# A hybrid mixer and attention block: weights split three groups ahead with five buffers per part, merge biases on SyncE's queue, and three small products in other forms

## The chip, the cores and the metric

The kernel runs on 1 core of one Trainium2 chip. The metric is the device time of one execution in microseconds, the median of several runs. The engines are TensorE (PE; its weight loads are PEld), VectorE (DVE), ScalarE (ACT), GpSimd (POOL) and SyncE (SP), which issues most DMAs.

## The reference

One layer: an RMS-normalised input, one wide input projection, two branches (an RWKV-7 time mixer and a banded attention over chunks of 64), each gated by SiLU and projected, a merge by sigmoid gates with a bias, an output projection and a second norm. x is 256 x 2048, float32.

```python
h = _rms_norm(x, pre_norm_g[l])
proj = h @ w_in[l]                       # 2048 x 12288
p_r, p_k, p_v, z_r, q_a, k_a_att, v_a, z_a, m_r, m_a = jnp.split(proj, split_points, axis=-1)
y_r = _rwkv7_mixer(h, p_r, p_k, p_v, ...) * jax.nn.silu(z_r)
y_a = _chunk_band_attention(q_a, k_a_att, v_a, rel_bias[l]) * jax.nn.silu(z_a)
u_r = y_r @ w_branch_rwkv[l]
u_a = y_a @ w_branch_attn[l]
merged = (jax.nn.sigmoid(m_r + b_merge[l, 0]) * u_r
          + jax.nn.sigmoid(m_a + b_merge[l, 1]) * u_a)
x = x + _rms_norm(merged @ w_out[l], post_norm_g[l])
```

In the mixer a recurrence over 256 steps keeps, for each of 16 heads, a 64 x 64 state; it is decayed by w = exp(-0.606531 sigmoid(w0 + tanh(xw @ w1) @ w2)), and the rate a = sigmoid(a0 + (xa @ a1) @ a2) enters it.

## The kernel before, in words

**Weights.** Every big matrix is streamed in pieces of 512 KB: SP issues the load into one of NR = 3 buffers (tag raw, L90 and L97), ACT copies it to a rounded high part wh (L81), DVE subtracts to get the low part wl (L82). Both parts have their own rings of NH = NL = 4 buffers. A big product is the sum of three products of parts: L275 does them token by token, L339 (wh, 512 columns) and L337 (wl, 256 columns) do them with the two parts of the activations side by side. A step of the plan is one piece of one matrix; `run_plan` prepares (loads and splits) pieces up to step n + 2 before it emits the products of step n.

**Accumulators.** The big products have two (pool pm, tag mm, the acc_ names); the small ones share four (pool ps, tag sm). After a big product, `take` reads its accumulator: ACT the one half (L381), DVE the other (L382), and the accumulator is free when DVE is through.

**Small products.** The mixer and the attention are generators whose pieces are emitted between the steps of the plan. Heads go in duos (j0 = 0, 2, 4, 6) and two groups g of eight heads. `group_decay` makes the decay's product lw from zw (L452), `duo_front` makes for each duo and m the products pc (L500) and pa (L506, the rate a, with 64 rows) and then a chain of DVE operations (L511 to L536) that fills AB. The chunk loop of a group goes over four chunks c: pw (L647, and L651 with the state SB), its copy W on ACT (L653), the transposes pt with their copy BT (L658, L659; for c < 3), pu (L663), its copy UV on DVE and ACT (L665, L666), py and pg (L672, L677, L680), then SB from pg on DVE (L688, L690) and Y from py on ACT (L691). Tiles of a group share buffers with later ones: the tile `late` (takes of attention's later q and k) lies in the buffer of A (tag A), which py reads.

**Order.** Each engine works through its own list in order. The lists are made at build time by the framework's scheduler, which lays out the emitted instructions by its own timing; so a changed dependency or buffer count can move work far from the edited line. PE, DVE, ACT and SP wait in place for what their next instruction needs.

**Merge.** For each of four column blocks c and both branches w, `load_bias` loads a 256 KB bias tile bb (tag bb) on ACT's queue (L952); as tag bb had no earlier user, the first two loads are issued near the start.

Of the kernel before, what the change touches and what calls it, by code (L numbers as in the profile page):

```python
# [24 lines left out]
NR = 3  # L25
NH = 4
NL = 4

# [9 lines left out]
P = 128  # L38
D = 2048
# [22 lines left out]
def kernel(ctx: ExitStack, tc, x, xt, vecs, w_in, wa1, w2, a2, w0, rel, w_br, w_ba, w_out, post_g, bm, out):  # L62
# [214 lines left out]
    def run_plan():  # L277
# [20 lines left out]
        for n, (q, g) in enumerate(steps):  # L298
            while ready < len(steps) and ready <= n + 2:
                prepare(ready)  # L300
                ready += 1
# [62 lines left out]
    def normalise():  # L364
# [101 lines left out]
    def duo_front(j0):  # L466
# [30 lines left out]
        for m in range(2):  # L497
            pc = small(f"pc{j0}{m}")
            for i in range(2):
                PE.matmul(pc[:, i * 130:(i + 1) * 130], d["s"][:, i, (q0 + m) * P:(q0 + m + 1) * P],  # L500
                          cum.rearrange("p c t -> p (c t)"), start=True, stop=True)
            pcv = pc[:, 0:260].rearrange("p (c t) -> p c t", c=4)
            ACT.activation(pp[:, 4 * m:4 * m + 4, :], pcv, AF.Exp, scale=-DECAY)
            ACT.activation(iv[:, 4 * m:4 * m + 4, :], pcv[:, :, 1:65], AF.Exp, scale=DECAY)
            pa = small(f"pa{j0}{m}")
            PE.matmul(pa[:, :T], RA[0][64:128, DB + (j0 + m) * P:DB + (j0 + m + 1) * P], za[64:128, :], start=True, stop=True)  # L506
            ACT.activation(ta[:, m, :], pa[:, :T], AF.Tanh, scale=0.5, bias=col(hv, H_A0 + j0 + m))
            yield
# [55 lines left out]
    def group_back(g):  # L564
# [71 lines left out]
        for q in range(2):  # L636
            ACT.activation(Rq[q][0:32, :, 32:64], p4[q][0:32, 0:256].rearrange("p (u t) -> p u t", u=8), AF.Copy)
            DVE.tensor_copy(Rq[q][64:96, :, 32:64], p4[q][64:96, 0:256].rearrange("p (u t) -> p u t", u=8))
        yield
        Y = bg.tile([P, 4, 4, C], F32, tag=("Y", "v")[g], name=f"Y{g}")  # L640
        d["Y"] = Y
        for c in range(4):
# [10 lines left out]
            ACT.activation(W.rearrange("p j t -> p (j t)"), pw[:, 0:256], AF.Copy)  # L653
            if c < 3:
                BT = tp.tile([P, 4, P], F32, tag="BT", name=f"BT{g}{c}")
                pt = small(f"pt{g}{c}")
                for jj in range(4):
                    PE.transpose(pt[:, jj * P:(jj + 1) * P], AB[jj // 2][:, jj % 2, c, 2:4, :].rearrange("p a t -> p (a t)"), ident)  # L658
                ACT.activation(BT.rearrange("p j t -> p (j t)"), pt, AF.Copy)  # L659
            pu = small(f"pu{g}{c}")  # L660
# [12 lines left out]
            if c < 3:  # L673
                pg = small(f"pg{g}{c}")
                for jj in range(4):
                    for h in range(2):
                        PE.matmul(pg[HS[h], jj * C:(jj + 1) * C], BT[:, jj, HS[h]], UV[:, h, jj, c, :], start=True, stop=True)  # L677
            for jj in range(4):
# [132 lines left out]
    def attend(j0, q, k, z):  # L811
# [32 lines left out]
        for m in range(2):  # L844
            j = j0 + m
            S = att[0][:, 2 * m:2 * m + 2, :]
            Pt = []
            for h in range(2):
                pT = small(f"pT{j}{h}")
                for b in range(3):  # L850
                    PE.transpose(pT[:, b * P:(b + 1) * P], S[:, h, b * P:(b + 1) * P], ident)
                t = att[1][:, 2 * m + h, :]
                ACT.activation(t, pT[:, 0:384], AF.Copy)
                Pt.append(t)
            yield
            po = small(f"po{j}")
            for h in range(2):
                vc = slice((2 * j + h) * C, (2 * j + h + 1) * C)
                PE.matmul(po[HS[h], 0:256], va[0][:, vc], Pt[h][:, 0:256], start=True, stop=False)
            for h in range(2):  # L860
                vc = slice((2 * j + h) * C, (2 * j + h + 1) * C)
                PE.matmul(po[HS[h], 128:256], va[1][:, vc], Pt[h][:, 256:384], start=False, stop=True)
            yg = tp.tile([P, T], F32, tag="rn", name=f"ya{j}", bufs=1)
            DVE.scalar_tensor_tensor(yg, po[:, :T], 0.5, z[:, m, :], op0=ALU.mult, op1=ALU.mult)
            split(ya[j // 4][:, j % 4, 0, :], ya[j // 4][:, j % 4, 1, :], yg)
            yield

# [30 lines left out]
    def project_za(j0):  # L898
        def done(acc):
            if j0 < 4:  # L900
                z = tp.tile([P, 2, T], F32, tag="BT" if j0 else "zs", name=f"za{j0}", bufs=2 if j0 else 1)
            else:
                z = place(2 + j0 // 2)
# [171 lines left out]
```

## Time and profile before

| | us |
|---|---|
| median of 3 runs | 866.53 (866.11 to 867.91) |
| the profiled execution | 866.37 |
| its span, first to last instruction | 864.7 |
| PE busy | 847.0 (98%) |
| DVE busy | 571.4 (66%) |
| ACT busy | 424.7 (49%) |
| POOL busy | 16.7 (2%) |
| chain of waits that ended last | PE 94%, DVE 2%, DMA 2%, ACT 1%, issue 1% |

The profiled execution's mean granted clock is 0.991. The largest waits of PE by the list of waits are 1.6 us each for a high part of r (near 10 us) and before lw (73 us), 1.3 for SB, 1.3 for a low part of the lora weights and 1.2 for W; everything else is below 1. In rows of the timeline, a row may stand for several instructions of one form ("x16"): its time is from the first one's start to the last one's end, and ends overlap the next row's start, so steps are measured from start to start.

### The profile page before, as it was taken

What the parts mean: (1) busy time and instruction counts of PE and PEld (TensorE: products, weight loads), DVE (VectorE), ACT (ScalarE), POOL (GpSimd) and SP (SyncE); (2) the same over time, 40 slices, a digit from 0 to 9 for tenths busy, and PEclk for the clock granted to TensorE, in tenths of its full rate; (3) what the DMA queues carried; (4) which work ended last, traced back from release to release, by engine and by line L of the source; (5) the groups of instructions that cost most, each with busy time, mean ns of one, the idle gap of its engine ahead of it and who ended that gap; (6) DMA issues with size and microseconds to landing.
All of it is one profiled execution on the core that took longest, in us unless ns stands there. A gap on an engine that the chain in (4) does not pass through costs nothing.

```text
span 864.7 us, 14000 instructions
## 1 busy us (share of the span) xinstructions
PE 847.0 (98%) x5624; PEld 716.0 (83%) x5624; DVE 571.4 (66%) x801; ACT 424.7 (49%) x600; POOL 16.7 (2%) x66
## 2 busy tenths in 40 slices
PE   8999999999999999999999999999999999999996
PEld 7997888888787888888887877888888888888896
DVE  6897996866759866644787864565554565555555
ACT  6567564535454444443476654434444434444433
POOL 2010000000010000000000000000000000000000
PEclk9999999999999999999999999999999999999998
DMA  9916535564134656643376445667666677676552
GB/s 284 266 50 183 177 116 154 178 173 133 54 118 146 178 155 179 197 123 120 91 236 189 129 134 167 205 193 204 205 194 193 205 206 229 214 245 203 194 190 98
DMA packets 119395, 149.35 MB, mean 173 GB/s; under 512 B 13601, under 2 KB 82209, under 8 KB 118946
## 3 DMA queue, kind: packets, MB, share of 16 engines
q1 hardware_dynamic: 105090, 138.43, 52.4%
q10 hardware_dynamic: 14240, 10.03, 4.2%
q8 instruction: 44, 0.72, 0.3%
q14 instruction: 21, 0.17, 0.1%
HBM read 145.82 MB, written 2.62 MB: 172 GB/s over the span
## 4 chain that ended last, share of the span: by engine, by line
PE 94%; DVE 2%; DMA 2%; ACT 1%; issue 1%; DVEq 0%; SPq 0%
PE acc_mr L275 10%; PE acc_ma L275 10%; PE acc_o L275 10%; PE acc_va L275 5%; PE acc_ua L275 5%; PE acc_ur L275 5%; PE acc_q L339 4%; PE acc_ak L339 4%; PE acc_zr L339 3%; PE acc_za L339 3%; PE acc_r L339 3%; PE acc_v L339 3%; PE acc_za L337 2%; PE acc_q L337 2%; PE acc_zr L337 2%; PE acc_ak L337 2%
## 5 line engine op out<-in xcount | busy, mean ns | idle before, releaser
L275 PE MATMUL acc_mr<-wh_mr,hn 128*128 128x512 f32 x256 | 80.9, 391 | 0.0
L275 PE MATMUL acc_ma<-wh_ma,hn 128*128 128x512 f32 x256 | 79.8, 390 | 0.0
L82 DVE TENSOR_TENSOR wl_ma<-raw_ma,wh_ma 128x1024 fp32r<-128x1024 f32 x32 | 39.2, 1225 | 42.7 <-ACT wh_ma L81 42.7
L82 DVE TENSOR_TENSOR wl_o<-raw_o,wh_o 128x1024 fp32r<-128x1024 f32 x31 | 37.9, 1225 | 35.0 <-ACT wh_o L81 35.0
L82 DVE TENSOR_TENSOR wl_mr<-raw_mr,wh_mr 128x1024 fp32r<-128x1024 f32 x32 | 39.2, 1224 | 30.0 <-ACT wh_mr L81 30.0
L275 PEld LDWEIGHTS acc_mr<-wh_mr,hn 128*128 128x128 f32 x256 | 48.1, 188 | 10.4 <-issue 0.7
L275 PEld LDWEIGHTS acc_ma<-wh_ma,hn 128*128 128x128 f32 x256 | 48.1, 188 | 10.3 <-issue 0.4
L81 ACT ACTIVATE wh_ma<-raw_ma 128x1024 fp32r<-128x1024 f32 x32 | 34.0, 1061 | 44.6 <-PE acc_ma L275 21.4
L81 ACT ACTIVATE wh_mr<-raw_mr 128x1024 fp32r<-128x1024 f32 x32 | 33.9, 1060 | 44.0 <-PE acc_ua L275 19.9
L81 ACT ACTIVATE wh_o<-raw_o 128x1024 fp32r<-128x1024 f32 x31 | 32.9, 1060 | 41.6 <-PE acc_o L275 25.7
L275 PE MATMUL acc_mr<-wl_mr,hn 128*128 128x512 f32 x128 | 50.1, 391 | 0.0
L275 PE MATMUL acc_ma<-wl_ma,hn 128*128 128x512 f32 x128 | 49.9, 390 | 0.0
L275 PE MATMUL acc_o<-wh_o,mgh 128*128 128x512 f32 (+1 forms) x140 | 49.9, 356 | 0.0
L275 PE MATMUL acc_o<-wl_o,mgh 128*128 128x512 f32 (+1 forms) x140 | 49.8, 356 | 0.0
L275 PE MATMUL acc_va<-wh_va,hn 128*128 128x512 f32 x128 | 40.7, 396 | 0.0
L339 PE MATMUL acc_ak<-hn,wh_ak 128*128 128x512 f32 x128 | 34.0, 400 | 0.0
L339 PE MATMUL acc_q<-hn,wh_q 128*128 128x512 f32 x128 | 33.6, 398 | 0.0
L339 PE MATMUL acc_zr<-hn,wh_zr 128*128 128x512 f32 x128 | 33.2, 396 | 0.0
L339 PE MATMUL acc_za<-hn,wh_za 128*128 128x512 f32 x128 | 32.6, 394 | 0.0
L82 DVE TENSOR_TENSOR wl_ua<-raw_ua,wh_ua 128x1024 fp32r<-128x1024 f32 x16 | 19.6, 1224 | 18.0 <-ACT wh_ua L81 18.0
L82 DVE TENSOR_TENSOR wl_ur<-raw_ur,wh_ur 128x1024 fp32r<-128x1024 f32 x16 | 19.6, 1224 | 17.9 <-ACT wh_ur L81 17.9
L82 DVE TENSOR_TENSOR wl_ak<-raw_ak,wh_ak 128x1024 fp32r<-128x1024 f32 x16 | 19.5, 1221 | 16.2 <-ACT wh_ak L81 15.1
(481 smaller groups left out, 2105.5 us busy)
## 6 DMA issues: line engine op xcount, KB each, us to landing
raw_mr<-w_in_d SPq DMA_DIRECT2D x32, 512.0 KB, 4.4
raw_ma<-w_in_d SPq DMA_DIRECT2D x32, 512.0 KB, 3.8
raw_o<-w_out_d SPq DMA_DIRECT2D x32, 512.0 KB, 4.6
raw_v<-w_in_d SPq DMA_DIRECT2D x16, 512.0 KB, 3.6
raw_q<-w_in_d SPq DMA_DIRECT2D x16, 512.0 KB, 4.1
raw_ak<-w_in_d SPq DMA_DIRECT2D x16, 512.0 KB, 3.7
raw_zr<-w_in_d SPq DMA_DIRECT2D x16, 512.0 KB, 4.0
raw_va<-w_in_d SPq DMA_DIRECT2D x16, 512.0 KB, 3.7
```

The source lines that it names most:

```text
L81: ACT.activation(h, src, AF.Copy)
L82: DVE.tensor_tensor(l, src, h.bitcast(F32), op=ALU.subtract)
L275: PE.matmul(d, u, v, start=first and n == 0, stop=last and n == len(ops) - 1)
L337: PE.matmul(acc[:, m, 0:256], wl[:, k, ms], a[:, 0, :], start=False, stop=g == ng - 1 and k == 3)
L339: PE.matmul(acc[:, m, :], wh[:, k, ms], a.rearrange("p n t -> p (n t)"), start=g == 0 and k == 0, stop=False)
```

## The change

Five edits:

- NH and NL go from 4 to 5, and pieces are prepared up to step n + 3.
- The product pa takes all 128 rows: the upper 64 rows of `za` and of its weights RA are set to zero on POOL.
- The transposes pt of all three chunks of a group come ahead of the chunk loop, into three buffers (BTs), which za2's gate tile shares.
- In attention the transposes pT of both m come first, then the products po of both, then what follows them on DVE and ACT.
- The merge biases use the buffers of the shift (tag xs, two) and SP's queue.

```diff
-NH = 4
-NL = 4
+NH = 5
+NL = 5
...
-            while ready < len(steps) and ready <= n + 2:
+            while ready < len(steps) and ready <= n + 3:
...
+        POOL.memset(RA[0][0:64, DB:2 * DB], 0.0)
...
+    POOL.memset(za[0:64, :], 0.0)
...
-            PE.matmul(pa[:, :T], RA[0][64:128, DB + (j0 + m) * P:DB + (j0 + m + 1) * P], za[64:128, :], start=True, stop=True)
+            PE.matmul(pa[:, :T], RA[0][:, DB + (j0 + m) * P:DB + (j0 + m + 1) * P], za, start=True, stop=True)
...
+        BTs = []
+        for c in range(3):
+            BTs.append(tp.tile([P, 4, P], F32, tag="BT", name=f"BT{g}{c}", bufs=3))
+            pt = small(f"pt{g}{c}")
+            for jj in range(4):
+                PE.transpose(pt[:, jj * P:(jj + 1) * P], AB[jj // 2][:, jj % 2, c, 2:4, :].rearrange("p a t -> p (a t)"), ident)
+            ACT.activation(BTs[c].rearrange("p j t -> p (j t)"), pt, AF.Copy)
+        yield
...
-            if c < 3:
-                BT = tp.tile([P, 4, P], F32, tag="BT", name=f"BT{g}{c}")
-                pt = small(f"pt{g}{c}")
-                for jj in range(4):
-                    PE.transpose(pt[:, jj * P:(jj + 1) * P], AB[jj // 2][:, jj % 2, c, 2:4, :].rearrange("p a t -> p (a t)"), ident)
-                ACT.activation(BT.rearrange("p j t -> p (j t)"), pt, AF.Copy)
...
+        po = [small(f"po{j0 + m}") for m in range(2)]
+        for m in range(2):
+            for n, c0, c1 in ((0, 0, 256), (1, 256, 384)):
+                for h in range(2):
+                    vc = slice((2 * (j0 + m) + h) * C, (2 * (j0 + m) + h + 1) * C)
+                    PE.matmul(po[m][HS[h], 128 * n:256], va[n][:, vc], att[1][:, 2 * m + h, c0:c1], start=not n, stop=bool(n))
+        yield
...
-                bb = tp.tile([P, 512], F32, tag="bb", name=f"bb{w}{c}")
+                bb = tp.tile([P, 512], F32, tag="xs", name=f"bb{w}{c}", bufs=2)
                 ts["b"] = bb
-                nc.scalar.dma_start(bb, bm[w * D + c * 512:w * D + (c + 1) * 512].partition_broadcast(P))
+                nc.sync.dma_start(bb, bm[w * D + c * 512:w * D + (c + 1) * 512].partition_broadcast(P))
```

Three places in the engines' lists follow. A row is the line, the operation, output<-inputs and the output's size; the last number of a name only numbers the tile. "x8" stands for eight instructions alike; a float32 product there runs as two in the trace.

**PE at the decay product lw, around 72 us, before.** acc_k2 is the third and fourth heads' k, hr its activations; lw00 needs zw; acc_r2 is the next big product.

```order
L275 MATMUL acc_k2_784<-hr_yrh_80,wl_k23_818 128x256
L275 MATMUL acc_k2_784<-hr_yrh_80,wh_k23_817 128x256 x2
L452 MATMUL lw00_809<-w2e_157,zw_158 128x512
L452 MATMUL lw01_813<-w2e_157,zw_158 128x512
L463 MATMUL pn0_860<-pn0h_856,onesr_112 128x512
L275 MATMUL acc_k2_784<-hr_yrh_80,wl_k23_818 128x256
L339 MATMUL acc_r2_966<-hn_655,wh_r20_876 128x512 x8
L337 MATMUL acc_r2_966<-hn_655,wl_r20_877 128x256
```

And after:

```order
L275 MATMUL acc_k2_791<-hr_yrh_80,wh_k23_785 128x256 x2
L275 MATMUL acc_k2_791<-hr_yrh_80,wl_k23_786 128x256
L339 MATMUL acc_r2_974<-hn_662,wh_r20_824 128x512 x7
L455 MATMUL lw00_816<-w2e_157,zw_158 128x512
L455 MATMUL lw01_820<-w2e_157,zw_158 128x512
L466 MATMUL pn0_868<-pn0h_864,onesr_112 128x512
L339 MATMUL acc_r2_974<-hn_662,wh_r20_824 128x512
L337 MATMUL acc_r2_974<-hn_662,wl_r20_825 128x256 x7
```

Seven products of acc_r2 now stand between the end of acc_k2 and lw.

**PE in group 0's chunk loop, around 220 us, before** (chunk 1; pw, pu, py, pg as above, and pt the transposes):

```order
L647 MATMUL pw01_1986<-UV0_850,A0_849 64x64 x8
L651 MATMUL pw01_1986<-SB_161,AB00_472 64x64 x4
L651 MATMUL pw01_1986<-SB_161,AB01_473 64x64 x4
L658 MATMUL pt01_2006<-ident_101,AB00_472 128x128 x2
L658 MATMUL pt01_2006<-ident_101,AB01_473 128x128 x2
L663 MATMUL pu01_2012<-W01_2003,RA_847 64x64 x8
L672 MATMUL py01_2023<-AB00_472,SB_161 64x64 x4
L672 MATMUL py01_2023<-AB01_473,SB_161 64x64 x4
```

And after:

```order
L337 MATMUL acc_ak0_2670<-hn_662,wl_ak03_2665 128x256 x8
L682 MATMUL pg00_1988<-UV0_858,BT00_1911 64x64
L685 MATMUL py00_1987<-A0_857,UV0_858 64x64
L682 MATMUL pg00_1988<-UV0_858,BT00_1911 64x64 x7
L685 MATMUL py00_1987<-A0_857,UV0_858 64x64 x7
L658 MATMUL pw01_2008<-UV0_858,A0_857 64x64 x8
L662 MATMUL pw01_2008<-SB_162,AB00_479 64x64 x4
L662 MATMUL pw01_2008<-SB_162,AB01_480 64x64 x4
L668 MATMUL pu01_2027<-W01_2025,RA_854 64x64 x8
L677 MATMUL py01_2066<-AB00_479,SB_162 64x64 x4
L677 MATMUL py01_2066<-AB01_480,SB_162 64x64 x4
```

No big product and no transposes stand any more between the end of acc_ak0 (the first row) and pg01.

**DVE at the same place, before** (SB the state; UV, AB, k and r as above; wl_zr23 and wl_va00 are low parts of weights):

```order
L82 TENSOR_TENSOR wl_zr23_2880<-raw_zr23_2881,wh_zr23_2879 128x1024
L525 SCALAR_TENSOR_TENSOR kk4_2172<-ta4_1894,kk4_2172 128x512
L665 COPY UV0_850<-pu01_2012 64x4x64
L527 SCALAR_TENSOR_TENSOR AB10_1229<-kk4_2172,iv4_1893 64x8x64 x2
L530 TENSOR_SCALAR ta4_1894<-ta4_1894,hv_154 128x256 x2
L688 TENSOR_TENSOR SB_161<-pg01_2032,SB_161 64x4x64 x2
L531 SCALAR_TENSOR_TENSOR k4_1368<-ta4_1894,k4_1368 128x512
L690 TENSOR_TENSOR SB_161<-SB_161,f0_476 64x4x64 x2
L533 TENSOR_TENSOR AB10_1229<-k4_1368,iv4_1893 64x8x64 x2
L536 SCALAR_TENSOR_TENSOR r4_1562<-r4_1562,vt_75,k4_1368 128x256 x2
L665 COPY UV0_850<-pu02_2108 64x4x64
```

And after:

```order
L528 SCALAR_TENSOR_TENSOR kk4_2149<-ta4_1902,kk4_2149 128x512
L82 TENSOR_TENSOR wl_va00_2888<-raw_va00_2889,wh_va00_2887 128x1024
L530 SCALAR_TENSOR_TENSOR AB10_1237<-kk4_2149,iv4_1901 64x8x64 x2
L533 TENSOR_SCALAR ta4_1902<-ta4_1902,hv_154 128x256 x2
L695 TENSOR_TENSOR SB_162<-pg00_1988,f0_483 64x4x64 x2
L534 SCALAR_TENSOR_TENSOR k4_1376<-ta4_1902,k4_1376 128x512
L536 TENSOR_TENSOR AB10_1237<-k4_1376,iv4_1901 64x8x64 x2
L539 SCALAR_TENSOR_TENSOR r4_1570<-r4_1570,vt_75,k4_1376 128x256 x2
L670 COPY UV0_858<-pu01_2027 64x4x64
```

The SB that pw01 waits for (from pg00) stood ahead of this piece and now stands behind wl_va00, L530 and L533.

**PE at the end of group 1's chunk loop, around 410 us, before** (acc_ak4 is attention's k of heads 8 to 11):

```order
L337 MATMUL acc_q4_4348<-hn_655,wl_q43_4382 128x256 x5
L339 MATMUL acc_ak4_4515<-hn_655,wh_ak40_4425 128x512 x8
L337 MATMUL acc_ak4_4515<-hn_655,wl_ak40_4426 128x256 x5
L680 MATMUL py13_3417<-A1_1876,UV1_1877 64x64
L337 MATMUL acc_ak4_4515<-hn_655,wl_ak40_4426 128x256 x2
L680 MATMUL py13_3417<-A1_1876,UV1_1877 64x64 x7
L337 MATMUL acc_ak4_4515<-hn_655,wl_ak40_4426 128x256
L339 MATMUL acc_ak4_4515<-hn_655,wh_ak41_4466 128x512 x8
L337 MATMUL acc_ak4_4515<-hn_655,wl_ak41_4467 128x256 x8
```

And after, at the end of the same loop:

```order
L685 MATMUL py12_3364<-A1_1884,UV1_1885 64x64 x7
L658 MATMUL pw13_3395<-UV1_1885,A1_1884 64x64 x5
L662 MATMUL pw13_3395<-SB_162,AB10_1237 64x64 x4
L662 MATMUL pw13_3395<-SB_162,AB11_1238 64x64 x4
L668 MATMUL pu13_3414<-W13_3412,RA_854 64x64 x8
L677 MATMUL py13_3443<-AB10_1237,SB_162 64x64 x4
L677 MATMUL py13_3443<-AB11_1238,SB_162 64x64 x4
L685 MATMUL py13_3443<-A1_1884,UV1_1885 64x64 x8
L339 MATMUL acc_q6_4623<-hn_662,wh_q60_4549 128x512 x8
```

On ACT there, after (W13, UV1 and Y1 belong to chunk 3; `late` takes acc_q4):

```order
L696 ACTIVATE Y1_3175<-py12_3364 128x4x64
L664 ACTIVATE W13_3412<-pw13_3395 128x256
L671 ACTIVATE UV1_1885<-pu13_3414 64x4x64
L696 ACTIVATE Y1_3175<-py13_3443 128x4x64
L383 ACTIVATE late_3588<-acc_q4_4356 128x512
```

py13's last half stood among acc_ak4's products; now all of chunk 3 from pw13 on stands behind acc_ak4, and acc_q6 right behind py13.

## Rows read from the trace of the kernel before

**Rows 1.** The page's busy times: engine, us, share of the span, instructions.

```profile
PE 847.0 (98%) x5624; PEld 716.0 (83%) x5624; DVE 571.4 (66%) x801; ACT 424.7 (49%) x600; POOL 16.7 (2%) x66
```

**Rows 2.** Table of stretches: us, busy time by engine, PEclk, DMA share, GB/s.

```profile
70.00:75.00 5.00, 3.42 (x17) 2.16 (x15) 3.74 (x5) 4.93 (x6) 0.10 (x1) 0.90 0.64 204
75.00:80.00 5.00, 5.00 (x22) 3.95 (x21) 3.46 (x8) 2.92 (x6) 0.10 (x1) 0.75 0.51 149
225.00:230.00 5.00, 3.84 (x68) 3.44 (x70) 4.63 (x10) 2.02 (x5) 0.00 (x0) 0.76 0.00 0
390.00:395.00 5.00, 5.00 (x53) 4.12 (x55) 2.70 (x5) 2.07 (x3) 0.00 (x0) 1.00 0.33 105
540.00:860.00 320.00, 316.76 (x1505) 266.39 (x1503) 174.73 (x163) 137.23 (x151) 1.36 (x1) 1.00 0.64 199
```

**Rows 3.** Timeline of the start: start, us, engine, line, operation [idle before].

```profile
58.06 0.69 DVE L379 TENSOR_TENSOR xsv<-acc_v,rones 128x512 f32<-128x512 f32 x1
...
57.06 0.38 PE L275 MATMUL acc_lora<-hr_yrh,wl_lora 128*128 128x256 f32 x1 [1.29 <-DVE wl_lora L82]
59.79 0.41 PE L275 MATMUL acc_k<-hr_A,wh_k 128*128 128x256 f32 x2
```

**Rows 4.** The same timeline at lw, ACT and PE.

```profile
70.04 1.06 ACT L81 ACTIVATE wh_r<-raw_r 128x1024 fp32r<-128x1024 f32 x1 [0.89 <-DMA raw_r<-w_in_d]
...
72.41 0.42 ACT L421 ACTIVATE zw<-lz 64x256 f32<-64x256 f32 x1
...
72.93 2.66 PE L452 MATMUL lw<-w2e,zw 65*128 65x512 f32 x4 [1.58 <-issue]
```

**Rows 5.** The same timeline of PE: pa, eight products, and full products pvr.

```profile
204.10 1.11 PE L337 MATMUL acc_ak<-hn,wl_ak 128*128 128x256 f32 x8
205.14 0.70 PE L506 MATMUL pa<-za,RA 64*128 64x256 f32 x2
205.77 0.49 PE L339 MATMUL acc_ak<-hn,wh_ak 128*128 128x512 f32 x1
...
208.92 1.10 PE L337 MATMUL acc_ak<-hn,wl_ak 128*128 128x256 f32 x8
209.86 1.09 PE L339 MATMUL acc_ak<-hn,wh_ak 128*128 128x512 f32 x4
...
415.26 1.89 PE L700 MATMUL pvr<-ysq,onesb 128*128 128x256 f32 x8
417.08 0.49 PE L822 MATMUL pS<-ak,aq 64*128 64x128 f32 x4
```

**Rows 6.** The same timeline in group 0's chunk loop, PE and DVE.

```profile
220.61 0.68 PE L663 MATMUL pu<-W,RA 64*64 64x64 f32 x16
221.22 0.69 PE L672 MATMUL py<-AB,SB 128*64 128x64 f32 x16
...
225.57 1.13 PE L651 MATMUL pw<-SB,AB 128*64 128x64 f32 x16 [1.33 <-DVE SB L690]
227.17 0.76 PE L663 MATMUL pu<-W,RA 64*64 64x64 f32 x16 [0.47 <-ACT W L653]
...
219.18 1.22 DVE L82 TENSOR_TENSOR wl_zr<-raw_zr,wh_zr 128x1024 fp32r<-128x1024 f32 x1
...
221.68 1.37 DVE L527 SCALAR_TENSOR_TENSOR AB<-kk,iv 64x512 f32<-64x512 f32 x2
...
223.60 0.86 DVE L688 TENSOR_TENSOR SB<-pg,SB 64x256 f32<-64x256 f32 x2
...
228.31 0.41 DVE L665 COPY UV<-pu 64x256 f32<-64x256 f32 x1
```

**Rows 7.** The same timeline in group 1's chunk loop, PE and ACT.

```profile
389.98 0.68 PE L663 MATMUL pu<-W,RA 64*64 64x64 f32 x16 [0.73 <-ACT W L653]
...
410.40 0.39 ACT L691 ACTIVATE Y<-py 128x256 f32<-128x256 f32 x1 [0.78 <-PE py L680]
410.68 0.59 ACT L381 ACTIVATE late<-acc_q 128x512 f32<-128x512 f32 x1
```

More of the change, by code (lines that the diff above doesn't have):

```diff
@@ L676, in group_back @@
                     for h in range(2):
-                        PE.matmul(pg[HS[h], jj * C:(jj + 1) * C], BT[:, jj, HS[h]], UV[:, h, jj, c, :], start=True, stop=True)
+                        PE.matmul(pg[HS[h], jj * C:(jj + 1) * C], BTs[c][:, jj, HS[h]], UV[:, h, jj, c, :], start=True, stop=True)
             for jj in range(4):
@@ L844, in attend @@
         for m in range(2):
-            j = j0 + m
             S = att[0][:, 2 * m:2 * m + 2, :]
-            Pt = []
             for h in range(2):
-                pT = small(f"pT{j}{h}")
+                pT = small(f"pT{j0 + m}{h}")
                 for b in range(3):
                     PE.transpose(pT[:, b * P:(b + 1) * P], S[:, h, b * P:(b + 1) * P], ident)
-                t = att[1][:, 2 * m + h, :]
-                ACT.activation(t, pT[:, 0:384], AF.Copy)
-                Pt.append(t)
+                ACT.activation(att[1][:, 2 * m + h, :], pT[:, 0:384], AF.Copy)
             yield
[L856 to L862, printed above, removed]
+        po = [small(f"po{j0 + m}") for m in range(2)]
[5 more added lines that the diff above has]
+        yield
+        for m in range(2):
+            j = j0 + m
             yg = tp.tile([P, T], F32, tag="rn", name=f"ya{j}", bufs=1)
-            DVE.scalar_tensor_tensor(yg, po[:, :T], 0.5, z[:, m, :], op0=ALU.mult, op1=ALU.mult)
+            DVE.scalar_tensor_tensor(yg, po[m][:, :T], 0.5, z[:, m, :], op0=ALU.mult, op1=ALU.mult)
             split(ya[j // 4][:, j % 4, 0, :], ya[j // 4][:, j % 4, 1, :], yg)
-            yield
+        yield
     tiles = {j0: {} for j0 in range(0, 8, 2)}
@@ L900, in done @@
             if j0 < 4:
-                z = tp.tile([P, 2, T], F32, tag="BT" if j0 else "zs", name=f"za{j0}", bufs=2 if j0 else 1)
+                z = tp.tile([P, 2, T], F32, tag="BT" if j0 else "zs", name=f"za{j0}", bufs=3 if j0 else 1)
             else:
```

## The prediction

> **What bounds the kernel now.** I read the page's busy times first: TensorE (PE) works 847.0 of 864.7 us [rows 1], so at most 17.7 us of the span are gaps, and everything else must come out of what the products themselves cost. Next I read the table of stretches [rows 2]. From 540 to 860 us PE is busy for 316.8 of 320 us at a granted clock of 1.00: no preparation of weights, however early, can gain anything there. The clock is below 1 in few places. From 70 to 80 us it is 0.90 and then 0.75, which makes 0.10 x 5 + 0.25 x 5 = 1.75 us of full speed lost; from 225 to 230 us it is 0.76. Both places lie right behind stretches in which PE waited. Last I read the timelines around PE's gaps, engine by engine, since each gap has its own releaser: the start [rows 3], the decay product lw [rows 4], the chunk loops of the mixer's two groups [rows 6, 7]. None of these gaps after 60 us is released by a weight of the big product that stands next; they are released by small results (zw, SB, W). So the deeper preparation can act only through the order in which engines come to these small results, and that is where I count.
>
> **The change part by part, gains.** *Start.* The first merge biases (256 KB each) are loaded on ACT's queue near the start, while the first weights are still on their way; in the new kernel they come far down SP's queue, between merge weights. Their bytes no longer compete with the first weights. What the start hands on is a chain on DVE from the norm's reciprocal to xsv at 58.06 [rows 3], whose end (58.06 + 0.69 = 58.75) frees the accumulator of acc_k. PE today reaches acc_k at 59.79, after waiting 1.29 for a low part of the lora weights. With that part split earlier, the wait goes and DVE's chain is what is late next: acc_k can start at about 58.75 - 0.1, a gain of **1.15 us**. If the chain itself comes 0.75 earlier the gain is 1.9; if DVE does the added early splits inside that chain (1.2 us each) it is nothing. I take 1.15, since the chain is nearest to the row that is there.
>
> *lw.* PE waits 1.58 at 72.93 for zw, which ACT makes at 72.41, behind a high part of r that waited for its raw weight until 70.04 [rows 4]. In the new order seven products of acc_r stand ahead of lw (7 x 0.23 = 1.6 us) and the weights of k are split earlier, so that SP can issue r's sooner. The wait should go: **1.6 us** (0 to 1.6). The lowered clock behind it goes too, **1.75 us** [rows 2] (0 to 1.75).
>
> *pa.* The 64-row product takes two passes: from 205.14 to 205.77 is 0.63, and the eight products before it, which take 0.94 from 208.92 to 209.86, take 1.04 from 204.10 to 205.14 when pa follows. Full 128-row products of the same 256 columns take (417.08 - 415.26) / 8 = 0.228, two of them 0.46 [rows 5]. So a pa saves 0.63 + 0.10 - 0.46 = 0.27, and eight of them **2.1 us** (1.4 without the 0.10). The two added memsets lie on POOL, which works 2% of the span [rows 1].
>
> The Trainium skill (TensorEngine Tiling (Array Packing), Theoretical Speedup) speaks against this edit: where the contraction has at most 64 rows it lists up to twice the speed of the full array. By it a pair would cost half of 0.46, and eight pairs would lose 0.23 each, 1.8 us, where I count a gain of 2.1. The rows show no such speed for a single 64-row product between full ones (0.63 against 0.46), so I give that outcome 3 in 100, at 872.0 us.
>
> **The change part by part, losses.** The order of PE is fixed at build time, and PE waits in it. *Group 0's chunk loop* (about 215 to 230 us). Before, the transposes pt stood between pw and pu and covered W's copy; still PE waits 1.33 and 0.47 there, 1.80 in all [rows 6]. Now pt comes first, pw01 to pu01 to py01 to pg01 follow with nothing between, and on DVE the state SB that pw01 needs stands behind wl_va00. That split reuses the fifth buffer back, which the last product of acc_ak0 frees. Counted from acc_ak0's end: the split, 1.22; then L530 to L539 with SB between, which are the seven DVE rows of the old kernel from 221.68 to 228.31 (6.63) without the second SB pair (0.86), 5.8; then the copy to UV, 0.41; about 7.5 with the hand-overs. PE has six steps of 16 small products to fill it, 0.61 each (220.61 to 221.22), 3.6. It waits about 3.9, and 0.2 more for ACT's half of UV: 4.1, against 1.80. **Loss 2.3 us** (1.1 if the split is done before acc_ak0 ends, up to 2.8). The low clock of 225 to 230 us stays.
>
> *Group 1's chunk loop* is moved later, against acc_ak2, acc_q4, acc_ak4 and acc_q6. The new waits: (a) acc_q4 needs acc_ak2's accumulator; DVE's take of it (0.69, as xsv's operation of that size [rows 3]) stands behind a split that waits for acc_ak2's end: 1.22 + 0.69 less pu10's 0.61, 1.3, less the 0.1 by which rows of DVE overlap, 1.2. (b) pw13 needs SB, two pairs of 0.86, behind a split, 1.22, 2.95 in all; PE has three small steps, 1.83: 1.1. (c) pu13 waits for W, 0.5, as the row of 0.73 at 389.98 and that of 0.47 show it [rows 6, 7]. (d) py13's second half waits for UV, 0.35. (e) acc_q6 needs acc_q4's accumulator, whose take writes `late`. That tile lies in A1's buffer, and py13 is A1's last reader. Behind py13 ACT copies Y (0.39), then takes half of acc_q4 (0.59), then DVE the other half (0.69) [rows 3, 7], and PE has nothing to do: 1.67, with the hand-overs 1.8. In the old order the same take, from 410.68 on, lay beside acc_ak's products. Sum 4.95, about 5.0, less today's 0.73: **loss 4.3 us** (2.0 without the two splits, up to 5.3). Four waits within some 6 us behind each other are more than the 1.33 and 0.47 after which the clock fell at 225 us, while after the 0.73 alone it stayed at 1.00 from 390 to 395 [rows 2, 7]: I add one more stretch of low clock, **1.75 us** (0 to 1.75).
>
> *At nothing:* attention's new order (pT of both m, then both po), since ACT's copies have big products beside them in both orders; uncovered it would be 0.5 a place, as for W above. The biases' loads on SP: they are issued several weights ahead of their use and their buffers, those of the shift, have long been read by then; the raw weights behind them on that queue are prepared well ahead in this part, the stretch from 540 us [rows 2].
>
> **The sum.** Against the profiled run's own 866.37: -1.15 - 1.6 - 1.75 - 2.1 = -6.6; + 2.3 + 4.3 + 1.75 = +8.35; together +1.75, so **868.1 us**. The median of the runs, 866.53, lies 0.16 above the profiled run. About 0.2%, 1.7 us, is what a measurement of this kernel tells from no change, so the sum stands on the edge of it.
>
> **The rivals.** *The clock holds.* If the waits in the chunk loops leave the granted clock at 1.00 in group 1 and in group 0 as well, 2 x 1.75 comes off: 864.6 (863 to 865.5). For it: the 0.73 at 389.98 had no fall behind it [rows 2]. Against it: group 0 fell after 1.80. *Slower, the early gain does not come.* The ring of raw weights keeps its three buffers. If SP's next raw weight waits for these and not for the parts, zw stays behind the same landing and lw waits as now; then 1.15, 1.6 and 1.75 are not gained: 872.6. It decides at lw: if PE still waits over 1 us there, this is the case. For it: wh_r waits for a raw weight today [rows 4]. Against it: seven products now stand ahead of lw. *The change does not reach.* The depth does nothing, since PE waits for no weight, and the new order's waits are covered: only pa counts, 866.37 - 2.1 = 864.3. Against it: the order does move, at the places shown.
>
> **How the numbers follow.** The forecast has 0.52, its own range 866.2 to 869.9 by the bounds of the two chunk loops; of that 0.26 is slower by over 0.2%, 0.23 within, 0.03 faster. The clock holds: 0.20 (0.17 faster, 0.03 within). No early gain: 0.17, slower. Not reached: 0.08 (0.06 faster, 0.02 within). The skill's speed: 0.03, slower. Together faster 0.26, within 0.28, slower 0.46. The range goes from 863.4, below the clock's and the third rival's time, to 872.2, which leaves out most of the case without the early gain.
>
> **What would show it.** In the new profile: no wait over 0.3 at the lora products and at lw, clock 1.00 from 70 to 80 us; pa rows of about 0.46 a pair; waits of SB before pw01 of some 2 us near 222; a wait of 1.5 to 2 us before acc_q6, released by DVE's `late`, with a clock below 1 behind it. Wrong would be: acc_q6 without a wait (then up to 4 us less), a wait left at lw (up to 4.5 more), or a weight (wh, wl) named as a releaser after 60 us, which I do not count at all.

## The result, and the profile after

The changed kernel takes 871.33 us (median of 6 runs, 868.73 to 873.32) against 866.32 (865.0 to 867.91) for the kernel before: ratio 1.0057, with an interval of 1.0036 to 1.0079. It is slower, by 3.1 to 6.8 us. The profiled execution took 872.91 us, 6.5 more than that of before.

The page's busy times, the line that answers to [rows 1]: engine, us, share of the span, instructions.

```profile
PE 848.3 (97%) x5624; PEld 718.5 (82%) x5624; DVE 570.5 (65%) x801; ACT 424.0 (49%) x600; POOL 18.8 (2%) x68
```

PE's work has hardly changed (848.3 for 847.0); the span has grown to 871.2, so the gaps grew from 17.7 to 22.9 us, and some of PE's busy time ran at the lower clock. The list of PE's waits names the gaps (who waits, for whom, us in total, times, longest):

```profile
PE pw L662 <- DVE SB L695: 3.2, 2, 2.2
PE acc_q L339 <- DVE late L384: 1.7, 1, 1.7
PE acc_ak L339 <- DVE aq L384: 1.6, 1, 1.6
...
PE acc_q L339 <- DVE ak L384: 1.5, 1, 1.5
PE xx L619 <- issue: 1.4, 1, 1.4
...
PE pu L668 <- ACT W L664: 0.9, 2, 0.5
```

The waits for the lora weights and for lw are gone; in their place stand five in the chunk loops and ahead of group 1's, none of them for a weight. Two of the lines left out are above 0.9: 1.5 for a high part of k near 7 us, where the kernel before waits 1.6 for one of r near 10 us, and 1.2 for wp at the very start, which both kernels have. The table of stretches shows what the clock did there (us, busy time by engine, PEclk, DMA share, GB/s), as [rows 2]:

```profile
70.00:75.00 5.00, 5.00 (x23) 3.61 (x23) 4.97 (x9) 4.58 (x8) 0.59 (x1) 1.00 0.69 213
75.00:80.00 5.00, 5.00 (x31) 4.46 (x30) 4.32 (x5) 4.96 (x8) 0.00 (x0) 1.00 0.66 206
215.00:220.00 5.00, 4.26 (x70) 3.82 (x72) 4.63 (x9) 2.22 (x5) 0.00 (x0) 0.58 0.06 21
220.00:225.00 5.00, 5.00 (x47) 4.45 (x44) 2.35 (x6) 1.44 (x3) 0.00 (x0) 0.74 0.01 3
...
380.00:385.00 5.00, 3.52 (x28) 2.74 (x28) 2.24 (x3) 1.38 (x4) 0.00 (x0) 0.80 0.49 164
385.00:390.00 5.00, 5.00 (x65) 4.19 (x64) 2.15 (x4) 1.93 (x3) 0.00 (x0) 0.86 0.02 6
...
420.00:425.00 5.00, 3.31 (x50) 2.96 (x47) 1.71 (x3) 2.77 (x6) 0.00 (x0) 0.56 0.01 4
425.00:430.00 5.00, 5.00 (x22) 4.16 (x22) 1.10 (x1) 2.17 (x2) 0.00 (x0) 0.76 0.00 0
540.00:860.00 320.00, 320.00 (x1507) 268.71 (x1507) 170.56 (x155) 137.61 (x148) 0.00 (x0) 1.00 0.60 197
```

*Where the time goes.* The big products are the same 3840 in both kernels and stand in nearly the same order, so the start of the same one in both traces tells how far ahead the new kernel is at that point (read only where the small work done before it is the same). It is 2.6 us ahead at the 400th product (61.71 before, 59.06 after), 7.4 at the 960th (177.32 and 169.88), 5.1 at the 1600th (344.83 and 339.75), and 6.9 behind at the 2000th (443.31 and 450.20); at the end it is 6.5 behind. So the early part gains 7.4, group 0's chunk loop gives back a net 2.4, and group 1's costs 12.0. The first of these holds for this one execution: seven kernels of the experiments have the same lists as the changed one on every engine up to the 960th product and reach it at 169.91 to 173.65 us, so the 7.4 is the best of eight, and the mean is 6.0. The step from the 1600th to the 2000th product is steadier: it takes 98.5 or 98.6 us in the kernel before and in all six whose group 1 begins where it did and whose transposes stay in the loop.

*The early part.* Timeline of after around the start and lw, as [rows 3, 4] (start, us, engine, line, operation [idle before <- releaser]):

```profile
56.25 0.68 DVE L381 TENSOR_TENSOR xsv<-acc_v,rones 128x512 f32<-128x512 f32 x1
...
57.08 0.47 PE L275 MATMUL acc_k<-hr_A,wh_k 128*128 128x256 f32 x2 [0.23 <-DVE xsv L381]
...
68.66 1.78 PE L339 MATMUL acc_r<-hn,wh_r 128*128 128x512 f32 x7
69.16 0.42 ACT L424 ACTIVATE zw<-lz 64x256 f32<-64x256 f32 x1
...
70.28 1.02 PE L455 MATMUL lw<-w2e,zw 65*128 65x512 f32 x2
```

DVE's xsv is ready at 56.25 instead of 58.06, acc_k follows at 57.08, and lw starts behind seven products of acc_r without any wait, since zw is ready at 69.58, 0.7 us ahead of it.

*Group 0*, as [rows 6]:

```profile
211.11 1.23 DVE L82 TENSOR_TENSOR wl_va<-raw_va,wh_va 128x1024 fp32r<-128x1024 f32 x1
...
214.18 0.87 DVE L695 TENSOR_TENSOR SB<-pg,f 64x256 f32<-64x256 f32 x2
214.64 1.14 PE L662 MATMUL pw<-SB,AB 128*64 128x64 f32 x16 [2.16 <-DVE SB L695]
...
216.25 1.12 PE L668 MATMUL pu<-W,RA 64*64 64x64 f32 x16 [0.47 <-ACT W L664]
...
218.59 0.47 PE L682 MATMUL pg<-UV,BT 128*64 128x64 f32 x2 [0.17 <-DVE UV L670]
```

SB stands behind the split of wl_va, and PE waits 2.16 + 0.47 + 0.17 = 2.8 us for 1.8 before.

*Group 1*, first in front of its chunk loop. Z is z masked, which xx multiplies with RA; RA, of which T is the transpose, comes by a load that both ACT and DVE wait for:

```profile
355.29 1.31 DVE L607 STREAM_TRANSPOSE T<-RA 128x512 f32<-128x512 f32 x2 [8.34 <-DMA RA<-rb]
356.52 3.46 DVE L82 TENSOR_TENSOR wl_ak<-raw_ak,wh_ak 128x1024 fp32r<-128x1024 f32 x3
359.89 1.28 DVE L615 TENSOR_TENSOR Z<-z,m 128x512 f32<-128x512 f32 x2
360.68 2.28 PE L619 MATMUL xx<-RA,Z 64*64 64x64 f32 x64 [1.39 <-issue]
361.56 1.06 ACT L81 ACTIVATE wh_q<-raw_q 128x1024 fp32r<-128x1024 f32 x1 [4.85 <-DMA raw_q<-w_in_d]
362.64 1.23 DVE L82 TENSOR_TENSOR wl_q<-raw_q,wh_q 128x1024 fp32r<-128x1024 f32 x1 [1.48 <-ACT wh_q L81]
363.79 0.68 DVE L384 TENSOR_TENSOR aq<-acc_q,aq 128x512 f32<-128x512 f32 x1
364.52 0.73 PE L339 MATMUL acc_ak<-hn,wh_ak 128*128 128x512 f32 x2 [1.57 <-DVE aq L384]
```

DVE waits 8.34 us for the load of RA, then does three splits of 1.15 that have piled up, and only then Z: xx waits 1.39. Then it waits for ACT's high part of q, whose raw weight ACT had waited 4.85 for, splits that too, and only then takes acc_q: acc_ak waits 1.57. Neither wait was in the prediction. Further on, in the chunk loop itself, come those that were:

```profile
380.79 1.23 DVE L82 TENSOR_TENSOR wl_ak<-raw_ak,wh_ak 128x1024 fp32r<-128x1024 f32 x1 [2.86 <-PE acc_ak L337]
382.04 0.69 DVE L384 TENSOR_TENSOR ak<-acc_ak,ak 128x512 f32<-128x512 f32 x1
382.79 1.47 PE L339 MATMUL acc_q<-hn,wh_q 128*128 128x512 f32 x3 [1.48 <-DVE ak L384]
...
418.18 1.13 PE L662 MATMUL pw<-SB,AB 128*64 128x64 f32 x16 [1.02 <-DVE SB L695]
...
422.56 0.38 ACT L696 ACTIVATE Y<-py 128x256 f32<-128x256 f32 x1 [1.21 <-PE py L685]
422.84 0.59 ACT L383 ACTIVATE late<-acc_q 128x512 f32<-128x512 f32 x1
...
423.46 0.69 DVE L384 TENSOR_TENSOR late<-acc_q,late 128x512 f32<-128x512 f32 x1 [2.52 <-ACT late L383]
...
424.20 1.65 PE L339 MATMUL acc_q<-hn,wh_q 128*128 128x512 f32 x3 [1.69 <-DVE late L384]
```

The waits of this group in the trace are 0.34 (z), 1.39, 1.57, 1.48, 1.02, 0.47 (W) and 1.69: 7.96, less the 0.73 of before [rows 7], 7.2. The clock below 1 from 380 to 390 and from 420 to 430 is worth (0.20 + 0.14 + 0.44 + 0.24) x 5 = 5.1, counted as if PE had worked all through. Together 12.3, for the 12.0 by which the products fall back.

### The profile page after: what moved, and what is told of

Read it like the earlier page. It is cut to its first block, busy times and chain, and to the rows that moved or that the text cites. A ratio compares the mean times of both kernels' runs of the same rounds, so it can differ in the third digit from the quotient of the medians.

```text
span 871.2 us, 14009 instructions
## 1 busy us (share of the span) xinstructions
PE 848.3 (97%) x5624; PEld 718.5 (82%) x5624; DVE 570.5 (65%) x801; ACT 424.0 (49%) x600; POOL 18.8 (2%) x68
## 4 chain that ended last, share of the span: by engine, by line
PE 55%; DVE 1%; ACT 0%; DVEq 0%; issue 0%
PE acc_mr L275 10%; PE acc_ma L275 10%; PE acc_o L275 9%; PE acc_ua L275 5%; PE acc_ur L275 5%; PE acc_q L339 2%; PE acc_za L339 2%; PE acc_ak L339 2%; PE acc_q L337 1%; PE acc_za L337 1%; PE acc_ak L337 1%; PE acc_zr L339 1%; PE po L862 1%; PE acc_last L275 1%; PE pT L854 1%; PE pS L829 1%
## 5 line engine op out<-in xcount | busy, mean ns | idle before, releaser
L339 PE MATMUL acc_q<-hn,wh_q 128*128 128x512 f32 x128 | 36.7, 427 | 3.2 <-DVE late L384 1.7
L339 PEld LDWEIGHTS acc_q<-hn,wh_q 128*128 128x128 f32 x128 | 24.6, 204 | 8.9 <-DVE late L384 1.9
```

The source lines that it names most:

```text
L339: PE.matmul(acc[:, m, :], wh[:, k, ms], a.rearrange("p n t -> p (n t)"), start=g == 0 and k == 0, stop=False)
```

## The experiments

The theory at the outset: the bias loads and the depth gain at the start, pa gains about 2, and the transposes ahead of the loop cause every loss. The rivals: the losses come from the depth (DVE's splits stand in other places), or the gains come from one edit alone. All times are medians; ratios are to runs of the kernel before on the same chip, and the us behind a ratio are worked out from it with 866.

### One part alone, and all but one

**Only the transposes.** The kernel before with BTs, the block of pt and the shared tag of za2, and nothing else.

```diff
+        BTs = []
+        for c in range(3):
+            BTs.append(tp.tile([P, 4, P], F32, tag="BT", name=f"BT{g}{c}", bufs=3))
...
+        yield
```

> The kernel before with one edit alone: the transposes pt ahead of the chunk loop (three buffers, shared with za2's gate). Theory: this edit alone makes the scheduler move both groups' small products, and all losses come from it. The changed kernel was 7.4 us ahead at 177 us and 6.5 us behind at the end, so the loss is about 13.9 us: 877 to 883 us, with waits of some 2 us before pw01 and before acc_q6 and clock below 1 behind them. Rival: the loss comes from the five buffers, whose splits wait for a product's end in the middle of DVE's chain; then this kernel, with four, is at 866 to 869 us.

878.55 us (876.17 to 881.22), ratio 1.0137 (1.011 to 1.0164): 11.9 us slower. Its waits of PE:

```profile
PE pw L659 <- DVE SB L692: 3.2, 2, 2.2
PE acc_q L339 <- DVE late L382: 1.7, 1, 1.7
PE acc_ak L339 <- DVE aq L382: 1.6, 1, 1.6
PE acc_q L339 <- DVE ak L382: 1.5, 1, 1.5
PE xx L616 <- issue: 1.4, 1, 1.4
```

The same five as in the changed kernel, to the tenth, with rings of four and depth two. So the depth has no part in them.

**All but the transposes.** The changed kernel with pt inside the loop again and without the block's `yield`.

```diff
-        BTs = []
-        for c in range(3):
-            BTs.append(tp.tile([P, 4, P], F32, tag="BT", name=f"BT{g}{c}", bufs=3))
...
-        yield
...
+            if c < 3:
+                BT = tp.tile([P, 4, P], F32, tag="BT", name=f"BT{g}{c}")
```

> The changed kernel with the transposes pt back in the chunk loop, all other edits kept. Theory: the gain of the first 177 us (7.4 us) stays and the chunk loops wait as in the kernel before: 857 to 861 us. Rival (five buffers cause the waits): 866 us or more, with the 2 us waits of pw01 and acc_q6 still there.

857.38 us (855.41 to 860.8), ratio 0.9896 (0.9867 to 0.9925): 9.0 us faster than before, and the fastest kernel seen. None of `late`, `aq`, `ak` and xx is in its list of waits. The transposes cost the changed kernel some 14 us (1.0057 - 0.9896 = 0.0161).

**Only the biases.** The kernel before with the three lines of bb.

```diff
-                bb = tp.tile([P, 512], F32, tag="bb", name=f"bb{w}{c}")
+                bb = tp.tile([P, 512], F32, tag="xs", name=f"bb{w}{c}", bufs=2)
...
-                nc.scalar.dma_start(bb, bm[w * D + c * 512:w * D + (c + 1) * 512].partition_broadcast(P))
+                nc.sync.dma_start(bb, bm[w * D + c * 512:w * D + (c + 1) * 512].partition_broadcast(P))
```

> The kernel before with the merge biases alone moved to the shift's buffers and SP's queue. Theory: this gives the start's part, 1.6 us by 30 us and no more than 2.6 by 60 us; lw's wait of 1.6 us and the low clock behind it stay: 863.7 to 864.9 us. Rival: the freed transfers alone make zw early too; then lw does not wait, and it is 860 to 862 us.

861.25 us (861.14 to 864.03), ratio 0.9943 (0.9925 to 0.9961): 4.9 us faster, more than the 1.1 to 2.3 expected. In its trace the lora wait is gone, xsv comes earlier than its 58.06 of before [rows 3], and lw waits 0.89 for 1.58 [rows 4]:

```profile
54.72 0.69 DVE L379 TENSOR_TENSOR xsv<-acc_v,rones 128x512 f32<-128x512 f32 x1
...
70.03 1.96 PE L452 MATMUL lw<-w2e,zw 65*128 65x512 f32 x4 [0.89 <-issue]
```

It is 4.5 us ahead at the 640th product (112.58 before, 108.07 here). In both kernels the 16 DMA engines are busy for nine tenths or more from 3.2 to 25 us, so the other loads lack what the biases take: the first lora weights land at 18.2 us here and at 21.4 in the kernel before, where the second bias lands ahead of them, at 14.0.

**The biases on ACT's queue.** The same buffers, but the loads stay on ACT's queue.

```diff
-                bb = tp.tile([P, 512], F32, tag="bb", name=f"bb{w}{c}")
+                bb = tp.tile([P, 512], F32, tag="xs", name=f"bb{w}{c}", bufs=2)
```

> The kernel before with the merge biases in the shift's buffers but still on ACT's queue, as against e3_only_bb. All eight loads then stand in the merge part of ACT's list. Theory: what counts is that 512 KB no longer land in the first 40 us, not the queue: the same as e3, 860 to 862.5 us, with no wait over 1 us at the lora products. Rival (SP's queue matters, since ACT's list is the one that waits): 864 to 867 us.

862.85 us (860.98 to 866.21), ratio 0.9972 (0.9954 to 0.999): 2.4 us faster by the medians, between what the theory and the rival had, with an interval that overlaps the last one's. In the trace the two are alike: xsv at 54.58, lw waiting 0.86, 5.4 us ahead for 5.2 at the end. What counts in the traces is when the load starts: with the shift's buffers the first bias is issued at 475.4 us here and at 472.1 there, in the kernel before at 4.2 us. That agrees with the Trainium skill (DMA: Bandwidth & Descriptors, Issuing engines are not separate DMA queues): the queue that issues a load gives it no engines of its own. The medians differ by more than the traces; whether the queue is worth the rest is open.

**Only the depth.** NH = NL = 5 and n + 3 in the kernel before.

```diff
-NH = 4
-NL = 4
+NH = 5
+NL = 5
...
-            while ready < len(steps) and ready <= n + 2:
+            while ready < len(steps) and ready <= n + 3:
```

> The kernel before with five buffers per part and preparation to step n + 3 alone. Theory: PE waits for no weight after 60 us, the start stays as loaded as before, and in this kernel's list lw stands seven products earlier than before, not later, so its wait stays or grows: 865.5 to 868.5 us. Rival: the depth alone takes away the waits at the lora products and at lw with the low clock behind it: 861 to 863 us.

865.96 us (864.45 to 869.3), ratio 1.0004 (0.9987 to 1.002): nothing. lw waits even longer, 2.52, and the clock behind it stays up:

```profile
70.00:75.00 5.00, 2.48 (x14) 1.67 (x13) 2.32 (x3) 3.85 (x5) 0.00 (x0) 1.00 0.63 195
75.00:80.00 5.00, 5.00 (x28) 3.99 (x26) 3.68 (x6) 4.20 (x6) 0.00 (x0) 1.00 0.55 175
```

PE works 2.48 of 5 us in the first stretch and is still granted 1.00; before, with 3.42 of 5, it was granted 0.90 and then 0.75 [rows 2].

**Only pa.** The kernel before with pa's 128 rows and the two memsets.

```diff
+        POOL.memset(RA[0][0:64, DB:2 * DB], 0.0)
...
+    POOL.memset(za[0:64, :], 0.0)
...
-            PE.matmul(pa[:, :T], RA[0][64:128, DB + (j0 + m) * P:DB + (j0 + m + 1) * P], za[64:128, :], start=True, stop=True)
+            PE.matmul(pa[:, :T], RA[0][:, DB + (j0 + m) * P:DB + (j0 + m + 1) * P], za, start=True, stop=True)
```

> The kernel before with the product pa over all 128 rows and the two memsets alone. Theory: 0.27 us for each of eight: 863.5 to 864.5 us (866.0 less 2.1), pairs of 0.46 us in the trace. Rival (a 64-row product runs at up to twice the speed, as the Trainium skill's page TensorEngine Tiling (Array Packing) lists it under Theoretical Speedup): about 867.8 us. Rival (hidden anyway): 866 us.

862.21 us (860.75 to 864.03), ratio 0.997 (0.9956 to 0.9983): 2.6 us faster; by the products' starts 2.8. Its timeline of PE at the place of [rows 5]:

```profile
202.75 1.12 PE L337 MATMUL acc_ak<-hn,wl_ak 128*128 128x256 f32 x8
203.71 0.60 PE L509 MATMUL pa<-za,RA 128*128 128x256 f32 x2
203.95 0.58 PE L339 MATMUL acc_ak<-hn,wh_ak 128*128 128x512 f32 x1
204.46 0.69 PE L650 MATMUL pw<-UV,A 128*64 128x64 f32 x16
```

The eight products ahead of pa take 0.96 (1.04 before), and from pa's start to that of pw, with one product of acc_ak between, is 0.75 us; in the kernel before it is 1.05 (205.14 to 206.19, where pw starts there). So a pa saves 0.38, and eight 3.0. The rule by which 64 rows would be faster, weighed in the prediction, does not hold for these single products between full ones.

### Which part of the transposes' move

The block does two things: it moves pt out of the loop, where it stood between pw and pu, and its `yield` adds one more piece to the generator that is emitted between the steps of the plan, so that every later piece of this branch comes later.

**Ahead in group 0 only, and in group 1 only.** The changed kernel with a condition on g; the other group keeps pt in the loop.

```diff
+        if g in (0,):
+            for c in range(3):
+                BTs.append(tp.tile([P, 4, P], F32, tag="BT", name=f"BT{g}{c}", bufs=3))
...
+            yield
...
+            if c < 3 and g not in (0,):
+                BTs.append(tp.tile([P, 4, P], F32, tag="BT", name=f"BT{g}{c}", bufs=3))
```

> The changed kernel with the transposes ahead of the loop in group 0 only; in group 1 they stay in the loop. In its list group 1's first products (z10, xx10) stand as late as in the changed kernel, and acc_q6 still follows py13 closely. Theory: group 0's moved transposes push group 1 later in the stream, and so most of group 1's loss comes from them: 866 to 870 us, with the waits before xx10 and acc_ak2 of 1.4 to 1.8 us each. Rival: each group's loss comes from its own transposes; then it is 859 to 861 us.

865.85 us (864.4 to 867.28), ratio 1.0004 (0.9989 to 1.0019). The list of waits has pw 2.2, `late` 1.7, `aq` 1.6 and xx 1.0: three of group 1's waits are there though group 1's code is the old one. The 1.5 for `ak` and the second wait of pw are not. From the 1600th to the 2000th product it takes 102.4 us, 3.9 more than the kernel before.

> The changed kernel with the transposes ahead of the loop in group 1 only. Group 0 and the place of z10 and xx10 are as in the kernel before, and ten big products stand between py13 and acc_q6. Theory: hardly any loss: 857 to 861 us, no wait over 1 us at xx10 and acc_ak2. Rival (each group's loss comes from its own transposes): 866 to 871 us.

858.05 us (857.17 to 858.51), ratio 0.9917 (0.9888 to 0.9945), hardly behind the kernel without the move (0.9896). No `late`, `aq`, `ak` or xx; only pg waits there, 1.3. So group 0's block is enough for three of group 1's waits, and group 1's own block alone makes none of the five: this damage is in what comes later, not where the transposes stand. The waits for `ak` (1.5) and for the second SB (1.0) come only in kernels with both blocks.

**An empty step.** The kernel with all but the transposes, and a bare `yield` at the block's place.

```diff
         yield
+        yield
         Y = bg.tile([P, 4, 4, C], F32, tag=("Y", "v")[g], name=f"Y{g}")
```

> The kernel of e2_all_but_pt (transposes inside the loop) with one empty step, a bare yield, ahead of the chunk loop, where the changed kernel has its step of transposes. No instruction is added. In its list z10, xx10 and the end of py13 stand exactly as late as in e5_pt_group0. Theory: the extra step, and not the transposes, pushes group 1 late; so the waits before xx10 (1.1 to 1.5 us), acc_ak2 (1.8) and acc_q6 (1.9) appear, less the 0.9 at pu12 that goes: 861 to 864 us against 857.4 of e2. Rival (the moved transposes themselves do it): 857 to 858.5 us.

862.97 us (861.64 to 865.4), ratio 0.9978 (0.996 to 0.9995): 7.1 us slower than without it (0.9978 - 0.9896; 4.6 by the profiled executions), though not one instruction was added. Three of group 1's waits are back:

```profile
PE acc_q L339 <- DVE late L384: 1.7, 1, 1.7
PE acc_ak L339 <- DVE aq L384: 1.7, 1, 1.7
...
PE xx L619 <- issue: 0.9, 1, 0.9
```

In the trace the product z of group 1 stands behind 1688 big products, as in the changed kernel; in the kernel before, and without the step, behind 1606. z starts at 342.47 us without the step and at 356.09 with it, and so the branch meets attention's q and k 14 us later. From the 1600th to the 2000th product it takes 102.4 us, 3.9 more than without the step, the same as with group 0's block.

**The transposes without the step.** The changed kernel without the block's `yield`.

```diff
             ACT.activation(BTs[c].rearrange("p j t -> p (j t)"), pt, AF.Copy)
-        yield
         Y = bg.tile([P, 4, 4, C], F32, tag=("Y", "v")[g], name=f"Y{g}")
```

> The changed kernel without the added yield: the transposes still come ahead of the loop, but in the same step as what follows. In its list z10 stands 49 big products earlier than in the changed kernel, between xx10 and acc_ak2 there are other products, and acc_q6 still stands right behind py13. Theory: the waits before xx10 and acc_ak2 (3.3 us) go, those of pw01 and acc_q6 stay: 866 to 868.5 us. Rival (the step does nothing): 870 to 872 us.

867.45 us (864.81 to 870.2), ratio 1.0018 (0.9996 to 1.004): 3.4 us better than the changed kernel. z stands behind 1639 products; the waits of xx and `aq` are gone or 0.3, `ak` is 0.5, but `late` waits 1.7, and in group 0's loop pw waits 2.4 and pg 1.6. So both halves of the edit hurt: 7.1 us for the step alone, 10.6 for the transposes alone (1.0018 - 0.9896), 13.9 for both. Whether they add is open: the 3.8 by which their sum is above 13.9 is what the intervals of the four ratios leave room for.

**One step fewer.** The kernel with all but the transposes, without the old `yield` ahead of the chunk loop.

```diff
-        yield
         Y = bg.tile([P, 4, 4, C], F32, tag=("Y", "v")[g], name=f"Y{g}")
```

> The kernel of e2_all_but_pt with one step less: the yield ahead of the chunk loop is dropped. In its list group 1 stands as in e2, and in group 0 pw00 to pw01 come earlier, with products of acc_ak0 between pw01's halves. Theory: the waits of pw02 for SB (1.3 us) shrink or stay, the rest is as in e2: 855.5 to 858 us. Rival (any change of steps costs waits): 860 us or more.

858.88 us (858.15 to 861.42), ratio 0.9931 (0.99 to 0.9962): no better than 857.38. Coming still earlier brings nothing; in group 0 pw waits 2.5 for SB, where the wait of 1.3 was expected to shrink or stay.

### The buffer of the last wait

**q4 in another buffer.** In the changed kernel, attention's q of heads 8 to 11 goes to a buffer of the shift instead of `late` in A1's, so that its take need not wait for py13.

```diff
+                elif j0 == 4 and what == "q":
+                    t = tp.tile([P, 2, T], F32, tag="xs", name="aq4", bufs=2)
```

> The changed kernel with one tile moved: attention's q of heads 8 to 11 is taken into a buffer of the shift (xs) and no longer into late, so acc_q6 need not wait for py13. In its list acc_q6's products now stand among the last chunk's steps. Theory: the waits before acc_q6 (1.95 us), pw13 (1.2) and pu13 (0.64) go and with them the low clock behind (1.75); acc_ak6, which takes the place right behind py13, gets about 1.3 us of wait: 866 to 869 us. Rival: the wait only moves to acc_ak6 and the clock falls there: 870 to 873 us.

869.1 us (867.85 to 873.32), ratio 1.0052 (1.0034 to 1.007), no measurable gain on 1.0057. The waits of acc_q6, pw13 and pu13 are gone, and the next one to use an A buffer has it: acc_ak waits 1.7 for `late`. The waits for xx, `aq` and `ak` are unchanged. Two lines of its table of stretches, in group 1:

```profile
375.00:390.00 15.00, 13.51 (x151) 11.29 (x151) 6.92 (x9) 6.75 (x11) 0.00 (x0) 1.00 0.34 108
410.00:435.00 25.00, 23.30 (x227) 19.61 (x223) 11.27 (x15) 11.45 (x16) 0.00 (x0) 1.00 0.40 128
```

The clock stays at 1.00 in both.

## Why the prediction was right or wrong

**The whole.** Slower was the likeliest case and the time lies in the range, but the sum of +1.75 was short: +5.0 by the medians, +6.5 by the profiled executions. The forecast's own range, 866.2 to 869.9, does not hold 871.33 (nor does it follow from the bounds given, which make 864.6 to 869.6). The whole range does hold it because it was drawn up to 872.2, towards the case without the early gain, which did not occur; that is luck. The early gain came about as sized, and one term, group 1, was half of what it is.

**Start and lw.** Predicted -1.15, -1.6 and -1.75; all three are there, no wait at lw, 0.23 at acc_k, clock 1.00 from 70 to 80 us. By 177 us the kernel is 7.4 ahead, and 6.0 in the mean of the eight with the same lists; the pa's among it are worth 1.2 (the kernel with pa alone is 1.19 ahead there), so 6.2, or in the mean 4.8, for the 4.5 predicted. The step that failed is its cause: I had put the lora split and lw down to the deeper preparation and had the biases only as bytes that no longer compete. The biases alone gain 4.9 and move xsv by 3.3 us; the depth alone gains nothing and leaves lw waiting 2.5. The 0.9 that lw still waits with the biases alone is gone in the changed kernel (0.3 and 0.6 are left in two of those with the same early lists); which of the other edits does that was not tried. The 1.15 was sized by PE's row at acc_k, when the whole of DVE's chain came earlier, by 1.81 in the changed kernel (58.06 to 56.25).

**pa.** Predicted 2.1, measured 2.6 to 2.8. The step that was mis-sized is what a 64-row pair costs its neighbours: only the products ahead of it were counted. The full pair, taken as 0.46, takes 0.43 where the next product's start shows it (115.39 to 115.82 in the kernel with pa alone). But the product behind the pair takes 0.42 before (205.77 to 206.19) and 0.32 here (0.75 less 0.43). Together the saving is 0.38 a place and not 0.27.

**Group 0.** Predicted a loss of 2.3. In the kernel with the transposes alone it is 2.1 (0.36 behind at the 960th product, 2.50 at the 1600th); that this comes near is luck, since the clock stays at 1.00 there from 215 to 235 us and the low clock of before is not in it. In the changed kernel the net is 2.4, but it contains the later pa's, worth 1.65 there in the kernel with pa alone, so the loss is about 4.0. Its waits are shorter than predicted (2.8, not 4.1); the clock, which I had left as it was, is lower: 0.58 and 0.74 are worth 3.4 us, before 0.76 and (from 230 to 235) 0.89 are worth 1.75. How the 4.0 divides beyond these two is not resolved. The reason given for the late split, the fifth buffer back, falls: with rings of four a split stands at the same place, and pw01 waits the same 2.16.

**Group 1.** Predicted 4.3 + 1.75, measured 12.0. The waits listed in the prediction came nearly as sized: acc_q4 1.48 for 1.2, pw13 1.02 for 1.1, W13 0.47 for 0.5, acc_q6 1.69 for 1.8, by the `late` that was named; only the 0.35 of py13 is missing. What failed is the list itself. I followed the chunk loop and not the steps ahead of it, though z and xx belong to the same generator and moved with it. There DVE's queue, held up by the load of RA and then by that of q, made 1.39 + 1.57 + 0.34 = 3.3 us of waits that I had not looked for. The other part is the clock: 5.1 us in two stretches for the 1.75 of one, in the execution with the lowest mean clock of the six (0.986).

**The cause.** I had described the later place of group 1 as the order's doing and priced its waits; that the extra `yield`, without the transposes, is enough to move it was not in the prediction. The empty step shows it, and it is worth 3.9 us of group 1's 12.0; the rest is further waits (`ak`, the second SB), which come only with both groups' blocks, and low clock. Why the one piece moves z by as many as 82 big products is not traced.

**The rivals.** *The clock holds*: not in the profiled execution. It does occur, since the kernel with q4 moved has four such waits without the falls in group 1; but its price, 1.75 a group, was low (5.1 in group 1), and its rule, and mine, that the size of the waits decides, was wrong. *The early gain does not come*: refuted, lw does not wait. *The change does not reach*: refuted by the waits. *64 rows are the faster form*: refuted, pa alone gains 2.6.

**Not tried:** attention's new order alone, and the biases with the depth. The kernel with all but the transposes gains 9.0, where biases, pa and depth alone gain 4.9 + 2.6 + 0 = 7.5; the 1.5 between them lies within the intervals.

## What to carry to other kernels

When pieces of a side branch are emitted between the steps of a plan, a new `yield` is not free: here it delayed all that the branch did later, and the price was paid far from the edit, so follow the branch's whole remainder in the new order, and look on each engine at what now stands ahead of the small results that PE waits for. A transfer that is needed late but has a free buffer starts early, and here the first loads landed later by it; giving it a buffer that comes free late was worth more here than two more weight buffers and a deeper preparation. Judge a bundle of edits one by one: four of these five together make the kernel 1% faster, and the fifth hides it.

## What was not expected of the hardware

The lowered clock does not follow from the size of a wait. A wait of 1.58 at lw was followed by 0.90 and 0.75 in the kernel before, one of 2.52 by 1.00 and 1.00 with the depth alone. Group 1's waits had clocks of 0.56 to 0.86 behind them in the changed kernel and 1.00 with q4 moved. The same 2.16 before pw01 was followed by 0.58 and 0.74 in the changed kernel and by 1.00 with the transposes alone. The mean clocks of the changed kernel's six runs go from 0.986 to 0.993, and their times from 868.73 (0.992) to 873.32 (0.988), though all have the same order of work. And a 64-row product costs its neighbours too: the eight full products ahead of it take 1.04 us, ahead of a 128-row one 0.96, and the one behind it 0.42 for 0.32.
